# Sparse attention of the odd layer: TensorE in a written order, the score matmuls regrouped by form

## The chip, the cores and the metric

The kernel runs on one core of a Trainium2 chip. The core has five engines that work from instruction queues of their own: TensorE (PE; its weight loads are listed as PEld), VectorE (DVE), ScalarE (ACT), GpSimd (POOL) and SyncE (SP, which here issues DMAs). The metric is the time of one execution on the device in microseconds (us); the median of several runs is quoted.

## The reference, cut to what matters

One sequence of T = 512 tokens, D = 1024, goes through two blocks. The first has two layers, an even one (pool and gated-unit mixer) and an odd one (sparse attention beside retention), each followed by a SwiGLU network; the second has dilated and forgetting attention and a mixture of experts. Only the sparse attention of the odd layer is touched:

```python
def nsa_attention(q, k_cmp, v_cmp, k_sel, v_sel, k_win, v_win, gates, ...):
    # 8 heads in 2 key groups of 4, head dim 64; queries in blocks of 128
    def block(i):                                   # tq: the block's 128 positions
        s = jnp.einsum('bgmqd,bgnd->bgmqn', qb, kc)              # 31 compressed keys
        p_cmp = masked_softmax(s, cmp_end[None, :] <= tq[:, None])
        o_cmp = jnp.einsum('bgmqn,bgnd->bgmqd', p_cmp, vc)
        ...                                          # top 16 blocks of 64 keys
        p = masked_softmax(s, tok_ok)
        o_sel = jnp.einsum('bgmqkl,bgqkld->bgmqd', p, vs)
        ...                                          # window of 512 keys
        o_win = jnp.einsum('bgmqs,bgsd->bgmqd', masked_softmax(s, win_ok), vwb)
        o = jnp.stack([o_cmp, o_sel, o_win], axis=-1)
        return jnp.einsum('bhqdc,bhqc->bqhd', o, gb)
    out = lax.map(block, jnp.arange(t_len // Q_BLOCK))
```

With 512 tokens the 16 chosen blocks and the window of 512 take in every earlier key, so that both branches are causal attention over different keys and values.

## The kernel before, in words

`nsa()` first projects and rotates queries, keys and values, and then runs the attention over `items`, nine for each of four query tiles `qt` of 128 tokens: one `compressed(qt)` and eight `selected(qt, br, b)`, for the two branches `br` (chosen keys, window) and four values of `b`. A selected item covers two heads (one of each key group `g`) and `nk = (qt + 1) * 128` keys: one block of 128 keys in the first tile, four in the last. Each item has three stages.

- `scores()` fills two PSUM tiles `mm` by matmuls: queries against the high part of the keys (`kh`, L840), queries against their low part, a 64-row matmul (`kl`, L844), and a bf16 matmul that adds the causal mask to the last 128 keys (`cmask`, L846). `soft` then has DVE take the row maximum (L892) and ACT the exponential (L902, tile `pe`).
- `turn()` transposes the two `pe` tiles on TensorE, 128x128 at a time (`keys_first`, L914, into PSUM `tp`), and copies them to `pt`, the first on ACT (L919), the second on DVE (L917).
- `values()` multiplies with the values (`pair_av`, L934, 64 columns a matmul) into a PSUM tile `px` that the four items of a branch share. After the fourth, `back()` copies `px` to `nat` on ACT (L940), transposes it by four matmuls on TensorE (L943); DVE scales it (L866, `ot`) and POOL adds it to `o` (L869). After the second branch `to_T` transposes `o` with four more matmuls (L199) and writes `mixa`, which the projection behind the attention reads.

A compressed item has scores on 31 keys (L794), a softmax of several DVE steps and one exponential (tile `ce`), transposes of `ce` (L813) and a matmul with `vbd` (L822) that starts `o`.

`staged()` writes the items with the lags `LAG = (0, 1, 2)`: scores of item n, transposes of n-1, values of n-2. That sets priorities only; a scheduler that works with its own model of durations chooses the order of the instructions on each engine. Every engine then executes its queue in that order, and waits on semaphores for what comes from others. Buffers: four `mm`, two `tp`, two `px` in PSUM, four `pe` and four `pt`.

Late in the last tile the scheduler also has matmuls of the projection behind (on `mixb`, L173 to L175) and the weight splits of the next stage (`whi`, ACT, L149) to place between.

Of the kernel before, what the change touches and what calls it, by code (L numbers as in the profile page):

```python
# [22 lines left out]
P = 128  # L23
# [55 lines left out]

HOLD_N = 8  # L80
UNITS = ("raw",) * 3 + ("more",) * 3 + ("whi", "wlo") * 3
LAG = (0, 1, 2)

QUOTA = ((16, 6.5), (26, 3.75), (35, 2.0))
G_CHUNK = [float(np.exp(P * np.log1p(-np.exp2(-5.0 - h)))) for h in range(4)]
# [6 lines left out]
class Builder:  # L92
# [555 lines left out]
    def nsa(self, np_, cp, h, mixp, mid):  # L648
        nc, A = self.nc, self.A
# [7 lines left out]
        kl = self.t(np_, "nkl", [P, 2, T], F32R)  # L657
# [21 lines left out]
        for tt in range(NT):  # L679
            cs = slice(tt * P, (tt + 1) * P)  # L680
            n = self.t(cp, "nat", [P, 512])
# [16 lines left out]
            for g in range(2):  # L698
                r = slice(64 * g, 64 * g + 64)
# [3 lines left out]
        for tt in range(NT):  # L703
            cs = slice(tt * P, (tt + 1) * P)
            n = self.t(cp, "nat", [P, 512])
# [6 lines left out]
            for g in range(2):  # L712
                r = slice(64 * g, 64 * g + 64)
# [12 lines left out]
        for i, nm in enumerate(("k", "v")):  # L726
# [10 lines left out]
            for lp in range(16):  # L737
                nc.tensor.matmul(ph[i][:, 0:93], w1[:, lp, :], x2[i][:, :, 2 * lp:2 * lp + 481:16], start=lp == 0,
                                 stop=lp == 15)
# [4 lines left out]
        q = self.t(aq, "nq", [P, 8, T], F32R)  # L744
        for tt in range(NT):
            cs = slice(tt * P, (tt + 1) * P)
            n = self.t(aq, "nat", [P, 512])
# [6 lines left out]
            for g in range(2):  # L754
                r = slice(64 * g, 64 * g + 64)
# [72 lines left out]
        def selected(qt, br, b):  # L828

            qs = slice(qt * P, (qt + 1) * P)  # L830
            nk = (qt + 1) * P
            key = (qt, br)
            st = {}

            def scores():
                if b == 0:
                    S[key] = [self.t(at, "sums", [P, 4, 2], bufs=2)]
                ps = [self.ps() for _ in range(2)]
                for g in range(2):
                    nc.tensor.matmul(ps[g][:, :nk], q[:, 4 * g + b, qs], kh[:, 2 * br + g, 0:nk], start=True,  # L840
                                     stop=False)
                for g in range(2):
                    r = slice(64 * g, 64 * g + 64)
                    nc.tensor.matmul(ps[g][:, :nk], q[r, 4 * g + b, qs], kl[r, br, 0:nk], start=False, stop=False)  # L844
                for g in range(2):
                    nc.tensor.matmul(ps[g][:, nk - P:nk], self.identb, self.cmask, start=False, stop=True)  # L846
                st["e"] = [self.soft(at, ps[g], None, nk, S[key][0][:, b, g:g + 1]) for g in range(2)]

            def turn():
                st["et"] = [self.keys_first(at, st["e"][g], nk, g) for g in range(2)]  # L850

            def values():
                if b == 0:
                    S[key].append(self.ps("px"))
                sums, av = S[key]
                self.pair_av(av[:, b * P:(b + 1) * P], st["et"], qt,
                             lambda g, kb: v[:, kb, br, g * 64:(g + 1) * 64])
                if b < 3:
                    return
                o = S[qt]  # L860
                cf = self.t(at, "scf", [P, 4, 2], bufs=2)
                nc.vector.reciprocal(cf, sums)
                nc.vector.tensor_tensor(cf, cf, gate[:, qt, 1 + br:24:3].rearrange("p (g b) -> p b g", g=2), op=ALU.mult)
                po = self.back(aq, av, ("nat", 1))
                t = self.t(at, "ot", [P, 512])
                nc.vector.tensor_tensor(t.rearrange("p (g b n) -> p b g n", g=2, b=4),  # L866
                                        po.rearrange("p (b g n) -> p b g n", g=2, b=4),
                                        cf.unsqueeze(3).to_broadcast([P, 4, 2, 64]), op=ALU.mult)
                nc.gpsimd.tensor_tensor(o, o, t, op=ALU.add)  # L869
                if br == 1:  # L870
                    self.to_T(o, qt, ma)

            return scores, turn, values

        items = []
        for qt in range(NT):
            items.append(compressed(qt))
            items += [selected(qt, br, b) for br in range(2) for b in range(4)]
        self.staged(items)
        self.done(at)  # L880
        self.done(aq)
        self.done(np_)
# [26 lines left out]
    def keys_first(self, pool, e, nk, odd):  # L909
# [8 lines left out]
        else:  # L918
            nc.scalar.activation(et[:, :nk], tp[:, :nk], AF.Copy)  # L919
        return et  # L920

    def staged(self, items, lag=LAG):

        items = list(items)
        for n in range(len(items) + lag[-1]):
            for k, d in enumerate(lag):
                if 0 <= n - d < len(items):
                    items[n - d][k]()

    def pair_av(self, av, et, qt, v):  # L930

# [1089 lines left out]
```

## Time and profile before

| | |
|---|---|
| median of 3 runs | 1884.65 us (1882.86 to 1886.02) |
| profiled execution | 1883.5 us, span 1881.8 us |
| mean granted TensorE clock | 0.971 of full |
| PE busy | 1786.6 us, 95% of the span |
| attention stage on PE, first compressed scores to first `mixa` matmul | 712.4 to 839.6 us |

The profiled execution lies inside the range of the runs, 1.15 us below their median. Times in the trace count from the start of the span. A busy time is the sum over instructions of an engine; matmuls overlap in the pipeline, so the step from the start of one group to the start of the next says what a group costs, and a row's duration is somewhat longer than that step. The granted clock has two levels, 0.50 (1.2 GHz) and 1.00 (2.4 GHz).

### The profile page before, as it was taken

Reading aid. Unit: us, or ns where it says so; the run is one execution under the profiler, and the core shown is the slowest. Engines: PE = TensorE matmul, PEld = TensorE weight load, DVE = VectorE, ACT = ScalarE, POOL = GpSimd, SP = SyncE. Lnnn points to the kernel's source line nnn. Section 1 sums busy time; section 2 is a strip of 40 time slices with the busy share of each in tenths; the row PEclk is TensorE's granted clock in tenths of the full one; section 3 lists DMA queues with packets and bytes.
Section 4 is the critical chain, followed back from the end, with each engine's and each line's share of the span. In section 5 each row is a group of like instructions: output and inputs, shape, how many; then the busy total and the mean of one; then the engine's idle time right before and its main releaser. Section 6 shows DMA issues by size and latency. Waiting matters only on the chain. (4 is left out here: it accounts for less than half of the span.)

```text
span 1881.8 us, 23441 instructions
## 1 busy us (share of the span) xinstructions
PE 1786.6 (95%) x9314; PEld 1367.1 (73%) x9315; DVE 922.6 (49%) x1637; ACT 626.5 (33%) x1152; POOL 164.6 (9%) x312
## 2 busy tenths in 40 slices
PE   8999999999999999999999999998999976999997
PEld 6788888888799876778888888876876763444443
DVE  7654444444645345555444444465455563334334
ACT  6333222222431334554322222245556421111112
POOL 1001000000232110002000000020000121000000
PEclk9999999999999996999999999999999986999999
DMA  6433223222331301043232232242312294999972
GB/s 231 148 134 132 93 90 105 97 90 90 111 125 56 90 25 44 1 144 103 90 112 90 90 111 90 68 140 87 92 46 83 80 339 176 374 369 376 348 305 86
DMA packets 136308, 257.01 MB, mean 137 GB/s; under 512 B 11319, under 2 KB 88023, under 8 KB 131971
## 3 DMA queue, kind: packets, MB, share of 16 engines
q1 hardware_dynamic: 124000, 231.89, 35.5%
q10 hardware_dynamic: 9282, 13.10, 2.1%
q0 software_dynamic: 2912, 10.49, 1.4%
q8 instruction: 75, 1.23, 0.3%
q14 instruction: 39, 0.31, 0.0%
HBM read 247.04 MB, written 11.03 MB: 137 GB/s over the span
## 5 line engine op out<-in xcount | busy, mean ns | idle before, releaser
L173 PE MATMUL mm<-acth,whi 128*128 128x512 f32 (+2 forms) x968 | 368.9, 381 | 0.0
L174 PE MATMUL mm<-actl,whi 128*128 128x512 f32 (+2 forms) x968 | 365.0, 377 | 0.0
L175 PE MATMUL mm<-acth,wlo 128*128 128x512 f32 (+2 forms) x968 | 364.4, 376 | 0.0
L150 DVE TENSOR_TENSOR wlo<-raw,whi 128x2048 fp32r<-128x2048 f32 (+1 forms) x96 | 218.7, 2279 | 247.6 <-ACT whi L149 247.4
L149 ACT ACTIVATE whi<-raw 128x2048 fp32r<-128x2048 f32 (+1 forms) x96 | 182.5, 1901 | 435.0 <-issue 195.2
L173 PEld LDWEIGHTS mm<-acth,whi 128*128 128x128 f32 (+1 forms) x968 | 182.0, 188 | 35.2 <-issue 2.4
L175 PEld LDWEIGHTS mm<-acth,wlo 128*128 128x128 f32 (+1 forms) x968 | 182.0, 188 | 34.5 <-issue 0.2
L174 PEld LDWEIGHTS mm<-actl,whi 128*128 128x128 f32 (+1 forms) x968 | 182.2, 188 | 33.6 <-issue 1.0
L173 PE MATMUL mm<-whi,acth 128*128 128x256 f32 (+2 forms) x480 | 160.2, 335 | 2.1 <-ACT gate L707 1.7
L174 PE MATMUL mm<-wlo,acth 128*128 128x256 f32 (+2 forms) x480 | 158.1, 330 | 0.6 <-DVE wlo L150 0.6
L175 PE MATMUL mm<-whi,actl 128*128 128x256 f32 (+2 forms) x448 | 145.6, 327 | 0.4 <-DVE actl L204 0.3
L173 PE MATMUL px<-whi,hidh 128*128 128x512 f32 x352 | 137.4, 390 | 0.6 <-DVE macc L331 0.6
L175 PE MATMUL px<-whi,hidl 128*128 128x512 f32 x352 | 137.9, 392 | 0.0
L174 PE MATMUL px<-wlo,hidh 128*128 128x512 f32 x352 | 137.4, 390 | 0.0
L331 DVE TENSOR_TENSOR macc<-px,macc 128x512 f32<-128x512 f32 x144 | 97.6, 688 | 75.3 <-PE px L175 75.3
L173 PEld LDWEIGHTS mm<-whi,acth 128*128 128x128 f32 x480 | 91.4, 191 | 10.2 <-ACT gate L707 1.9
L174 PEld LDWEIGHTS mm<-wlo,acth 128*128 128x128 f32 x480 | 91.2, 190 | 8.4 <-DVE wlo L150 1.3
L175 PEld LDWEIGHTS mm<-whi,actl 128*128 128x128 f32 x448 | 85.1, 190 | 7.2 <-DVE actl L204 1.0
L173 PEld LDWEIGHTS px<-whi,hidh 128*128 128x128 f32 x352 | 66.1, 188 | 16.4 <-DVE macc L331 1.5
L311 DVE TENSOR_TENSOR hidf<-mm,silu 128x512 f32<-128x512 f32 x44 | 30.4, 690 | 94.8 <-PE mm L175 94.8
L175 PEld LDWEIGHTS px<-whi,hidl 128*128 128x128 f32 x352 | 66.1, 188 | 14.1 <-DVE hidl L313 0.5
L174 PEld LDWEIGHTS px<-wlo,hidh 128*128 128x128 f32 x352 | 66.1, 188 | 13.2
(427 smaller groups left out, 2683.8 us busy)
## 6 DMA issues: line engine op xcount, KB each, us to landing
raw<-in_ffn_w_gate SPq DMA_DIRECT2D x22, 1024.0 KB, 5.2
raw<-in_ffn_w_up SPq DMA_DIRECT2D x22, 1024.0 KB, 5.3
raw<-in_ffn_w_down SPq DMA_DIRECT2D x22, 1024.0 KB, 4.8
mixd<-in_w_expert_down SPq DMA_DIRECT2D x16, 1024.0 KB, 6.9
down<-in_w_expert_down SPq DMA_DIRECT2D x16, 1024.0 KB, 9.1
raw<-in_od_w_in SPq DMA_DIRECT2D x12, 1024.0 KB, 5.0
raw<-in_w_expert_gate SPq DMA_DIRECT2D x18, 512.0 KB, 8.4
raw<-in_w_expert_up SPq DMA_DIRECT2D x18, 512.0 KB, 8.3
```

Source lines behind the costliest of these rows:

```text
L149: self.nc.scalar.activation(hi[:, :n], raw[:, :n], AF.Copy)
L150: self.nc.vector.tensor_tensor(lo[:, :n], raw[:, :n], hi[:, :n].bitcast(F32), op=ALU.subtract)
L173: mm(out, l[0], r[0], start=first, stop=False)
L174: mm(out, l[0], r[1], start=False, stop=False)
L175: mm(out, l[1], r[0], start=False, stop=last)
L311: nc.vector.tensor_tensor(hf, pu[f], s, op=ALU.mult)
L331: nc.vector.tensor_tensor(m, p, m, op=ALU.add)
```

## The change

In `scores()` the two mask matmuls come between those of the high part and those of the low part, which are now last. The items are written out under a manual schedule for PE: TensorE's instructions are executed in exactly the order in which the code writes them. In step n that order is the transposes of item n-2, the scores of item n, and the values of item n-2. `staged` and `LAG` go. The orders of DVE and ACT are still chosen by the scheduler, around the new order of PE; the orders of SP and POOL are the same rows as before. Lines move by a few: `kh` L839, `cmask` L842, `kl` L845, exponential L908, transposes L920, `pt` L923 and L925, values L932, `nat` L938, `back` L941, `to_T` L198, `ce` transposes L812.

```diff
@@ scores
                 for g in range(2):
+                    nc.tensor.matmul(ps[g][:, nk - P:nk], self.identb, self.cmask, start=False, stop=False)
+                for g in range(2):
                     r = slice(64 * g, 64 * g + 64)
-                    nc.tensor.matmul(ps[g][:, :nk], q[r, 4 * g + b, qs], kl[r, br, 0:nk], start=False, stop=False)
-                for g in range(2):
-                    nc.tensor.matmul(ps[g][:, nk - P:nk], self.identb, self.cmask, start=False, stop=True)
+                    nc.tensor.matmul(ps[g][:, :nk], q[r, 4 * g + b, qs], kl[r, br, 0:nk], start=False, stop=True)
@@ the loop over the items
-        self.staged(items)
+        with self.tc.manual_schedule(engines={mybir.EngineType.PE}):
+            for n in range(len(items) + 2):
+                if n >= 2:
+                    items[n - 2][1]()
+                if n < len(items):
+                    items[n][0]()
+                if n >= 2:
+                    items[n - 2][2]()
@@ gone
-LAG = (0, 1, 2)
-    def staged(self, items, lag=LAG):
-        items = list(items)
-        for n in range(len(items) + lag[-1]):
-            for k, d in enumerate(lag):
-                if 0 <= n - d < len(items):
-                    items[n - d][k]()
```

**The end of a first branch.** The first place is TensorE in the third tile (three blocks of keys), where the first branch (`br` 0) ends. Before, behind the last values of that branch (into `px_6364`), these rows stood:

```order
L840 MATMUL mm_6487<-nkh_4825,nq_5552 128x384
L840 MATMUL mm_6488<-nkh_4825,nq_5552 128x384
L844 MATMUL mm_6487<-nkl_4826,nq_5552 128x384
L844 MATMUL mm_6488<-nkl_4826,nq_5552 128x384
L846 LDWEIGHTS identb_79
L846 MATMUL mm_6487<-cmask_81,identb_79 128x128
L846 LDWEIGHTS identb_79
L846 MATMUL mm_6488<-cmask_81,identb_79 128x128
L914 MATMUL tp_6503<-ident_72,pe_6449 128x128 x3
L943 MATMUL px_6479<-ident_72,nat_6477 128x128 x4
L914 MATMUL tp_6509<-ident_72,pe_6453 128x128 x3
```

Now the same place, from the last two of the branch's last six values matmuls (into `px_6354`) on; ahead of the six stand the `kl` scores of `mm_6442` and `mm_6443`:

```order
L932 MATMUL px_6354<-pt_6434,v_4827 64x128
L932 MATMUL px_6354<-pt_6440,v_4827 64x128
L941 MATMUL px_6469<-ident_72,nat_6467 128x128 x4
L920 MATMUL tp_6477<-ident_72,pe_6417 128x128 x3
L920 MATMUL tp_6483<-ident_72,pe_6421 128x128 x3
L839 MATMUL mm_6489<-nkh_4825,nq_5552 128x384
L839 MATMUL mm_6490<-nkh_4825,nq_5552 128x384
```

The transposes of `back` (of `nat`) stood a whole scores group and three transposes behind the values whose result they need; now they stand directly behind them. The same has happened at the ends of the other branches.

**The end of a tile.** The second place is TensorE at the end of the second branch of the same tile, where `o` (`o_6014` before, `o_6006` now) is finished. Before:

```order
L943 MATMUL px_6288<-ident_72,nat_6286 128x128 x4
L822 MATMUL px_6332<-vbd_5487,ct_6277 128x256 x2
L840 MATMUL mm_6337<-nkh_4825,nq_5552 128x384
L844 MATMUL mm_6337<-nkl_4826,nq_5552 128x384
L846 LDWEIGHTS identb_79
L846 MATMUL mm_6337<-cmask_81,identb_79 128x128
L840 MATMUL mm_6371<-nkh_4825,nq_5552 128x384
L840 MATMUL mm_6372<-nkh_4825,nq_5552 128x384
L199 MATMUL tp_6296<-ident_72,o_6014 128x128 x4
L914 MATMUL tp_6319<-ident_72,pe_6267 128x128 x3
```

Now:

```order
L932 MATMUL px_6172<-pt_6252,v_4827 64x128
L932 MATMUL px_6172<-pt_6257,v_4827 64x128
L941 MATMUL px_6285<-ident_72,nat_6283 128x128 x4
L198 MATMUL tp_6293<-ident_72,o_6006 128x128 x4
L812 MATMUL tp_6300<-ident_72,ce_6234 128x128 x2
L839 MATMUL mm_6305<-nkh_4825,nq_5552 128x384
```

The transposes of `o` stood six matmuls of the next tile and the values of its compressed item behind those of `nat`; now nothing stands between them. The same holds at the end of the first two tiles; at the end of the last tile the `mixb` matmuls of the projection still stand between.

**The copy that `back` waits for.** The third place is ACT around the copy `nat` at the first place. Now:

```order
L925 ACTIVATE pt_6434<-tp_6430 128x384
L908 ACTIVATE pe_6451,sums_6407<-mm_6442,nm_6450 128x384
L908 ACTIVATE pe_6455,sums_6407<-mm_6443,nm_6454 128x384
L938 ACTIVATE nat_6467<-px_6354 128x512
L925 ACTIVATE pt_6481<-tp_6477 128x384
```

The copy `nat` stands behind both exponentials of the scores `mm_6442` and `mm_6443`, which TensorE computes directly before the last values. Before, `nat_6477` stood behind the two exponentials of the preceding scores in the same way.

## Rows read from the trace of the kernel before

**Rows 1.** The page, part 1: busy time, share of the span, instructions.

```profile
PE 1786.6 (95%) x9314; PEld 1367.1 (73%) x9315; DVE 922.6 (49%) x1637; ACT 626.5 (33%) x1152; POOL 164.6 (9%) x312
```

**Rows 2.** Windows of the stage: length; busy PE, PEld, DVE, ACT, POOL; granted clock; DMA.

```profile
712.30:729.30 17.00, 13.88 (x58) 11.34 (x58) 11.40 (x38) 7.92 (x23) 0.00 (x0) 0.50 0.12 44
729.40:739.50 10.10, 10.07 (x83) 7.30 (x82) 4.80 (x21) 5.97 (x28) 1.26 (x1) 1.00 0.01 2
739.60:753.10 13.50, 13.50 (x53) 8.95 (x51) 6.97 (x18) 5.38 (x18) 1.27 (x1) 0.50 0.00 0
753.30:839.60 86.30, 84.93 (x676) 61.61 (x676) 52.00 (x102) 47.64 (x123) 7.69 (x6) 1.00 0.21 73
```

**Rows 3.** Waits of PE in the stage: line and releaser, us in total, times, longest.

```profile
PE tp L199 <- POOL o L869: 1.1, 3, 0.6
```

**Rows 4.** Timeline of PE, one item of three blocks: start, us, work [idle before].

```profile
783.52 0.61 PE L840 MATMUL mm<-nkh,nq 128*128 128x384 f32 x2
784.07 0.44 PE L844 MATMUL mm<-nkl,nq 64*128 64x384 f32 x2
784.45 0.29 PE L846 MATMUL mm<-cmask,identb 128*128 128x128 bf16 x2
784.57 0.82 PE L914 MATMUL tp<-ident,pe 128*128 128x128 f32 x6
785.32 0.88 PE L934 MATMUL px<-pt,v 128*64 128x128 f32 x12
786.13 0.44 PE L840 MATMUL mm<-nkh,nq 128*128 128x384 f32 x1
```

**Rows 5.** Timeline of PE where scores follow transposes.

```profile
761.15 0.60 PE L914 MATMUL tp<-ident,pe 128*128 128x128 f32 x4
761.51 0.36 PE L840 MATMUL mm<-nkh,nq 128*128 128x256 f32 x1
```

**Rows 6.** Timeline of DVE and ACT beside and behind rows 4.

```profile
784.71 1.02 DVE L892 TENSOR_REDUCE nm<-mm 128x1 f32<-128x384 f32 x2 [1.12 <-PE mm L846]
785.55 0.57 ACT L902 ACTIVATE pe<-mm,nm 128x384 f32<-128x384 f32 x1
786.10 0.58 ACT L902 ACTIVATE pe<-mm,nm 128x384 f32<-128x384 f32 x1
786.66 0.60 ACT L940 ACTIVATE nat<-px 128x512 f32<-128x512 f32 x1
```

**Rows 7.** Timeline of PE at a tile's end, transposes of `nat` and of `o`.

```profile
771.95 0.60 PE L943 MATMUL px<-ident,nat 128*128 128x128 f32 x4
774.77 0.44 PE L199 MATMUL tp<-ident,o 128*128 128x128 f32 x2 [0.24 <-POOL o L869]
```

**Rows 8.** Timeline of PE, from one compressed item's values to the next's.

```profile
772.39 1.03 PE L822 MATMUL px<-vbd,ct 128*128 128x256 f32 x4
791.77 1.96 PE L794 MATMUL mm<-kcT,nq 128*128 128x32 f32 x16
799.47 0.38 PE L822 MATMUL px<-vbd,ct 128*128 128x256 f32 x1
```

**Rows 9.** Timeline of PE at the start of the stage.

```profile
723.88 0.47 PE L840 MATMUL mm<-nkh,nq 128*128 128x128 f32 x1 [3.06 <-ACT pe L902]
```

**Rows 10.** Timeline of PE: the same scores at either clock level.

```profile
740.33 0.80 PE L840 MATMUL mm<-nkh,nq 128*128 128x256 f32 x2
758.28 0.50 PE L840 MATMUL mm<-nkh,nq 128*128 128x256 f32 x2
```

**Rows 11.** Timeline and windows around two stretches where PE stood idle.

```profile
1639.54 0.63 PE L1675 MATMUL tp<-ident,xg 128*128 128x128 f32 x4 [1.06 <-ACT wsl L1650]
1640.70:1644.00 3.30, 3.14 (x10) 1.48 (x12) 0.20 (x1) 0.70 (x2) 0.00 (x0) 0.50 0.96 307
666.00:668.00 2.00, 0.31 (x2) 0.22 (x2) 1.97 (x2) 1.70 (x3) 1.71 (x1) 1.00 0.00 0
668.00:675.00 7.00, 6.28 (x36) 4.85 (x35) 5.57 (x28) 3.10 (x12) 2.20 (x6) 1.00 0.42 150
```

## The prediction

> **What bounds the kernel now.** I read the page first: TensorE (PE) is busy for 95% of the span [rows 1], so time is won or lost where PE's groups get shorter or where PE stands still. Then the windows of the attention stage, which alone is touched. PE is granted half of its clock for the first 17 us, the full clock for 10, half again for 13.5, and the full clock for the last 86.3, of which it is busy 84.93 [rows 2]. So before the change PE hardly waits in the stage, although every item passes through DVE and ACT between its matmuls; the waits of PE name only the transposes of `o`, 1.1 us in three places [rows 3]. Last the timeline of one item of three blocks: from one score group to the next are 2.61 us: high part 0.55, low part 0.38, mask 0.12, transposes 0.75, values 0.81 [rows 4]. That is matmul after matmul, and the other engines' work lies under it.
>
> **The regrouping.** No matmul is added or removed; only neighbours change. In rows 4 the six transposes take 0.75 us up to the values, which are about 0.11 a step and 0.20 for the last, since a matmul of another shape of the array (64 columns) follows. Where high-part scores follow four transposes, the four take 0.36 [rows 5], three steps of 0.11 and a last one of 0.03. In the new order scores follow the transposes in every item: minus 0.17. The transposes now follow the values instead of the mask; I take 0.05 more for that, an estimate from the first step of the values, which is longer by about as much than the later ones. The mask followed by another score group instead of transposes: about minus 0.02. Sum minus 0.14 us an item, and about the same at one, two and four blocks since only borders change: 32 items, **minus 4.4 us** (bounds minus 5, without the 0.05 and a little more, and minus 1, if the low part pays at its border with the values what the transposes saved).
>
> A page bears on this. The Trainium skill, "TensorEngine Tiling (Array Packing)", section "Key Properties", says that a change of the tiling mode drains TensorE. An item had four such changes and has three, so by the page one border an item goes, which at the 0.09 us by which the border step exceeds the others would be minus 2.9 us, between my bounds. The row does not show a drain as such, only the longer step.
>
> **The written order at the ends of branches.** This is the large term. Before, the transposes of `nat` stood a score group and some transposes behind the values that they wait for, and PE did not wait there; now they stand directly behind. In the new order ACT copies `nat` behind both exponentials of the scores that PE finishes just before these values. For three blocks, counted from the start of the values, t: the first maximum can start when the low part ends, t + 0.06; one maximum is 0.51 (half of the pair's 1.02), and with 0.14 to the exponential, an estimate, the first exponential starts at t + 0.71; the two exponentials take 0.55 each from start to start, and `nat` starts at t + 1.81; its 0.60 and an estimated 0.07 to PE give t + 2.48 [rows 6]. PE is through the values at t + 0.81 [rows 4]. It waits 2.48 - 0.81 = 1.67 us. With fewer keys the exponentials and the values both get shorter; I work out 1.4 for one block and 1.6 for two, and 2.1 for four, where a weight split of ACT can stand between: **6.8 us for the four first branches**. At the ends of the first three tiles the scores ahead are the next tile's and one exponential fewer stands ahead of `nat`: I take 0.85, 1.35 and 1.35, **3.5 us**. At the end of the last tile matmuls of the projection still cover it, at nothing; without that cover it would be another 1.5.
>
> Behind `back`, at the ends of the first three tiles, PE comes at once to the transposes of `o`. These wait for DVE's scaling and POOL's addition. Before, from the start of the transposes of `nat` to those of `o` passed 2.82 us, of which PE waited 0.24, since it had the compressed values and scores to do meanwhile [rows 7]. That time was set by POOL, so it stays; PE's own part of it is now the four transposes alone, 0.44 (771.95 to 772.39, [rows 7, 8]). It waits 2.82 - 0.44 = 2.38 us, three times: **7.1 us**. The matmuls that covered it still have to be done afterwards. Stalls together **plus 17.4 us** (bounds 13.6, with each `nat` a row of 0.55 earlier and nothing at the first tile, and 19).
>
> **What the written order removes.** The waits of 0.24 and its like at the ends of the first three tiles are inside the 2.82 now: **minus 0.5 us** (the last tile's 0.6 stays). And the scheduler's order was irregular at the ends of tiles, with single score matmuls between others. From the values of one compressed item to the next in the third tile pass 27.08 us (772.39 to 799.47). Eight items of 2.61 make 20.9, the scores of the compressed item 1.9, its transposes and values 0.9, two backs 0.9, the transposes of `o` 0.45, and 0.6 more for the scores of the next tile that fall inside with four blocks: 25.7 [rows 4, 7, 8]. The 1.4 left over, three times, is **minus 4.2 us** (bounds minus 6 and 0, if the surplus belongs to the work and not to its order).
>
> **The start.** Before, PE had scores of two and a half items to do before it stood still for 3.06 us on the exponentials that free its buffers [rows 9]; in the new order it has one item's scores and then the transposes of `ce`, behind the softmax of the compressed item. Both orders wait for that chain. The scores that were done early come later: one and a half items at one block, at half clock about 1 us each, **plus 1.5 us** (bounds 0 and plus 3).
>
> **The clock.** The same pair of scores takes 0.80 us at half and 0.50 at full clock [rows 10], a ratio of 1.6. The half stretch of 13.5 us [rows 2] thus costs 13.5 x (1 - 1/1.6) = 5.1 us. An idle time of 1.06 us late in the kernel is followed by some 3.4 us at half clock, which by the same ratio costs 1.3; but an idle time of 1.69 us (most of the window from 666 to 668) is followed by the full clock [rows 11]. Seven stalls of the new order could each bring such a stretch, plus 9; or the stretch of 13.5 us may not come back, minus 5. The rows bear out both kinds; I take **plus 2 us**, near the middle.
>
> **The sum.** -4.4 + 17.4 - 0.5 - 4.2 + 1.5 + 2 = +11.8 us on the profiled 1883.5: **1895 us**, slower by 0.6%. The profiled execution lies 1.15 us below the median of its runs, so that on the median the sum would be 1896.5; I stay with 1895.
>
> **Rivals.** What a measurement of this kernel can tell from no change is about 0.2%, 3.8 us.
>
> 1. *PE does not stand still at the moved transposes, and the kernel is faster.* If ACT and DVE run so far ahead of PE that `nat` and `o` are ready in time, the stalls fall away and the sum is -5.6: about 1878 us, or 1871 if the half stretch goes too. It decides if the stalls are below 5.6 us. For it: ACT is busy for 47.64 of 86.3 us [rows 2] and could copy `nat` earlier. Against it: the order has `nat` behind both exponentials, and POOL's addition was waited for even with cover [rows 3]. The Trainium skill ("TensorE: Matmul & The Clock Gate", section "Part 3: Packing small matmuls — row/col tiling") says that matmuls keep strict program order; the trace agrees as far as PE stood idle 0.24 us before the transposes of `o`. Chance 0.08.
> 2. *The clock stays full* from 729 on, in spite of the stalls: -5.1 in place of +2, 1888 us. For it: the stalls are short and the idle of 1.69 us did no harm [rows 11]. Chance 0.15.
> 3. *The stalls hold the clock down*: the full stretch of 10.1 us [rows 2] at half, 10.1 x 0.6 = +6.1, and half stretches behind most stalls, +3.5 more: 1905 us. For it: the stalls in the first two tiles come while the clock goes up and down anyway. Chance 0.14.
> 4. *The regrouping saves nothing*: stalls as forecast, 1899.5 us. As a mechanism: the weights of the first scores cannot be loaded under the last transpose, so that the border costs what the border to the values cost. The 0.03 in rows 5 speak against it. The same page and section of the Trainium skill have weight loads overlap running matmuls only where the row group differs, which is not so between transposes and scores; that is this rival, and row and rule differ here. Chance 0.06.
>
> **How the numbers follow.** The forecast has 0.57; its own range, from the bounds of stalls, surplus and start, is 1889 to 1901. The range of 1886 to 1905 leaves out the first rival and about half of the third, and a little of the forecast: 0.2. Faster than 1881 us: the first rival, 0.08. Within 0.2%, up to 1888.4: rather more than half of the second and a little of the forecast, 0.13. Slower: 0.79.
>
> **What would show it.** In the new profile the seven transposes of `nat` outside the last tile's end should have idle time before them released by ACT (`nat`), 1.3 to 2.1 us at first branches, and the transposes of `o` three waits on POOL of 2.2 to 2.5 us; PE's waits in the stage should come to some 17 us more than before. Six transposes followed by scores should take about 0.6 us, an item of three blocks 2.46. From the values of the third tile's compressed item to those of the fourth's [rows 8] should pass some 3 us more. I am wrong above all if `nat` is ready much sooner than t + 2.48, if the scheduler's surplus was worth more than 4 us, or if the clock in the first two tiles goes another way.

## The result, and the profile after

The changed kernel took 1903.04 us (median of 5 runs, 1894.88 to 1905.46) against 1884.2 us before (median of 5 too, the three of the table ahead and two more): 18.8 us more between the medians. The ratio over all runs is 1.0081, 95% interval 1.0063 to 1.0100, which is 12 to 19 us. Runs of either kernel scatter by several us with the granted clock (one set of 30 runs of the kernel before goes from 1881.6 us at a mean of 0.973 to 1892.3 at 0.965, and 1894.88 us is the one run of the changed kernel at 0.971, the other four being at 0.965), so kernels are compared below by the ratio to runs of the kernel before on the same chip.

The page of the changed kernel, part 1, answers to [rows 1]:

```profile
PE 1791.6 (94%) x9314; PEld 1371.8 (72%) x9315; DVE 926.6 (49%) x1637; ACT 626.7 (33%) x1152; POOL 162.4 (9%) x312
```

The same matmuls are busy for 5 us more in a span that is 21.7 us longer (1903.5): PE stands still more, and its matmuls are on the mean slower. Where it waits says the view of PE's waits in the attention stage (line and releaser, us in total, times, longest), which answers to [rows 3]:

```profile
PE px L941 <- ACT nat L938: 10.0, 7, 2.5
PE tp L198 <- POOL o L868: 7.1, 4, 2.2
PE tp L812 <- ACT ce L801: 4.1, 1, 4.1
```

Seven waits on `nat` and four on the sum `o`; the fourth of the latter, 0.6 us, was there before. The third row is the wait at the start, which was 3.06 us before [rows 9]. How fast PE ran shows in the windows of the stage (columns as in [rows 2], which they answer to):

```profile
55.30:62.10 6.80, 6.80 (x17) 4.39 (x15) 6.37 (x7) 0.60 (x1) 0.22 (x3) 0.50 0.44 157
717.50:761.80 44.30, 36.14 (x173) 28.25 (x173) 21.18 (x65) 16.95 (x61) 2.53 (x2) 0.50 0.02 8
761.90:785.70 23.80, 18.89 (x174) 14.57 (x172) 13.31 (x35) 11.81 (x42) 2.53 (x2) 1.00 0.00 1
785.80:789.10 3.30, 3.30 (x12) 2.50 (x11) 2.28 (x4) 1.51 (x6) 0.00 (x0) 0.50 0.00 0
789.20:816.40 27.20, 22.08 (x214) 17.02 (x212) 15.74 (x35) 13.49 (x39) 2.54 (x2) 1.00 0.01 2
816.50:819.80 3.30, 3.30 (x11) 1.88 (x11) 1.98 (x3) 1.35 (x3) 0.00 (x0) 0.50 0.00 0
819.90:860.30 40.40, 37.22 (x290) 27.44 (x289) 22.91 (x31) 20.67 (x42) 2.58 (x2) 1.00 0.42 149
```

The clock is at half from the start of the stage to the end of the first tile, 44.3 us in one piece; the full stretch of 10 us that stood between two half ones in [rows 2] is gone. Half stretches come again behind the waits at the ends of the second and the third tile. The first row lies far ahead of the stage and is one of the clock's changes from run to run (below).

The stage itself, from the first compressed scores to the first `mixa` matmul, runs from 716.4 to 860.4 us, these rows of PE's timeline:

```profile
716.37 0.28 PE L793 MATMUL mm<-kcT,nq 128*128 128x32 f32 x1 [0.56 <-ACT kcT L767]
...
860.40 0.39 PE L172 MATMUL mm<-whi,mixa 128*128 128x512 f32 x1
```

It takes 144.0 us, and took 127.2 (712.4 to 839.6): 16.8 of the 22.0 us between the two profiled executions (1905.46 and 1883.5). PE's busy time in it is the second number of these windows, the first of the kernel before and the second of the changed one:

```profile
712.40:839.60 127.20, 122.74 (x866) 89.29 (x867) 75.27 (x177) 66.95 (x190) 10.23 (x8) 0.88 0.16 55
716.40:860.40 144.00, 121.99 (x867) 92.51 (x868) 78.52 (x177) 66.71 (x190) 10.18 (x8) 0.82 0.14 48
```

PE is busy for as long as before and stands idle for 22.0 us where it was 4.5.

One item of three blocks gives the answer to [rows 4]:

```profile
791.12 0.88 PE L920 MATMUL tp<-ident,pe 128*128 128x128 f32 x6
791.75 0.60 PE L839 MATMUL mm<-nkh,nq 128*128 128x384 f32 x2
792.19 0.28 PE L842 MATMUL mm<-cmask,identb 128*128 128x128 bf16 x2
792.40 0.44 PE L845 MATMUL mm<-nkl,nq 64*128 64x384 f32 x2
792.77 0.88 PE L932 MATMUL px<-pt,v 128*64 128x128 f32 x12
793.58 0.88 PE L920 MATMUL tp<-ident,pe 128*128 128x128 f32 x6
```

From transposes to transposes 2.46 us, where it was 2.61: in step starts, 0.63 for the six transposes and their border to the scores (0.75 before).

The chain behind a first branch's last values, with the same columns, on three engines; it answers to [rows 6]:

```profile
797.70 0.88 PE L932 MATMUL px<-pt,v 128*64 128x128 f32 x12
797.80 1.02 DVE L898 TENSOR_REDUCE nm<-mm 128x1 f32<-128x384 f32 x2 [0.28 <-PE mm L845]
798.45 0.58 ACT L908 ACTIVATE pe<-mm,nm 128x384 f32<-128x384 f32 x1 [0.84 <-DVE nm L898]
799.02 0.57 ACT L908 ACTIVATE pe<-mm,nm 128x384 f32<-128x384 f32 x1
799.58 0.59 ACT L938 ACTIVATE nat<-px 128x512 f32<-128x512 f32 x1
800.23 0.66 PE L941 MATMUL px<-ident,nat 128*128 128x128 f32 x4 [1.65 <-ACT nat L938]
```

PE's values end at 798.6; `nat` could be copied from then on, but ACT has two exponentials ahead of it in its queue, the first of which waits for DVE. PE comes to the transposes 2.53 us after the values began.

The end of a tile, the answer to [rows 7]:

```profile
812.87 0.66 PE L941 MATMUL px<-ident,nat 128*128 128x128 f32 x4 [1.27 <-ACT nat L938]
813.64 0.69 DVE L865 TENSOR_TENSOR ot<-px,scf 128x512 f32<-128x512 f32 x1 [1.32 <-PE px L941]
814.41 1.26 POOL L868 TENSOR_TENSOR o<-o,ot 128x512 f32<-128x512 f32 x1 [11.38 <-DVE ot L865]
815.72 0.55 PE L198 MATMUL tp<-ident,o 128*128 128x128 f32 x3 [2.19 <-POOL o L868]
```

From one group of transposes to the other 2.85 us, 2.82 before, and now all but PE's own part of it is idle.

### The profile page after: what moved, and what is told of

It reads as the page before. It is cut to its first block, busy times and chain, and to the rows that moved or that the text cites. A ratio compares the mean times of both kernels' runs of the same rounds, so it can differ in the third digit from the quotient of the medians.

```text
span 1903.5 us, 23434 instructions
## 1 busy us (share of the span) xinstructions
PE 1791.6 (94%) x9314; PEld 1371.8 (72%) x9315; DVE 926.6 (49%) x1637; ACT 626.7 (33%) x1152; POOL 162.4 (9%) x312
## 4 chain that ended last, share of the span: by engine, by line
PE 26%; issue 20%; DVE 3%; ACT 2%; POOL 1%; DMA 0%; POOLq 0%; ACTq 0%; DVEq 0%
PE mm L1686 5%; PE mm L1709 4%; PE px L1727 3%; PE mm L172 3%; PE mm L174 3%; PE mm L173 3%; PE px L932 1%; PE tp L920 1%; PE tp L1673 1%; PE sc L1198 1%; PE sc L1192 1%; POOL rq L214 0%; DMA xg<-hd,ix 0%; DVE hn L240 0%; PE tp L1639 0%
```

## The experiments

**The changed kernel again**, unaltered.

> The changed kernel once more, beside the others of this call on the same chip: 1895 to 1906 us, as in its five runs. The first profile has 16.8 of its 22 us in the attention stage and 4 us ahead of it, where no instruction differs. Theory: the 4 us are the clock's (6.8 us at half clock near 55 us) and differ from run to run; rival: they belong to the change and come again.

1901.82 us (5 runs), ratio 1.0070 (1.0046 to 1.0093). The stage begins at 711.97 us, not at 716.37, and takes 143.0 us: the 4 us ahead of the stage do not belong to the change (the half stretch of 6.8 us there is worth 2.6 of them by the forecast's ratio), and some 16 us in the stage do. The clock in the first tile is not the same as in the first profile of this kernel:

```profile
712.00:729.00 17.00, 12.36 (x56) 10.48 (x56) 10.98 (x35) 7.25 (x18) 0.00 (x0) 0.50 0.11 42
729.10:735.80 6.70, 4.86 (x47) 3.51 (x43) 2.65 (x13) 4.22 (x20) 0.00 (x0) 1.00 0.00 1
735.90:756.30 20.40, 17.48 (x83) 13.53 (x82) 8.94 (x24) 6.45 (x25) 2.53 (x2) 0.50 0.00 1
```

Here the full clock came back for 6.7 us, and fell again behind the wait of 1.39 us on `nat` that ended at 735.15 us. Half clock in the whole stage comes to some 48 us here, 51 in the first profile and 31 before.

**Only the regrouping**, with the scheduler's order: the edit of `scores()` in the diff, made in the kernel before.

> The kernel before, with only the mask matmuls moved ahead of the low part; the scheduler chooses the order. The number of borders between array shapes stays the same in that order, four an item (high to low part, low part to transposes, transposes to values, values to scores), so my theory gives no change: 1882 to 1886 us. Rival (the regrouping itself saves, or costs, at every item): 4 us or more to either side.

1883.55 us, ratio 0.9994 (0.9978 to 1.0010): no change, as expected. In the scheduler's order the regrouping bought nothing.

**Only the written order**:

```diff
+                    r = slice(64 * g, 64 * g + 64)
+                    nc.tensor.matmul(ps[g][:, :nk], q[r, 4 * g + b, qs], kl[r, br, 0:nk], start=False, stop=False)
+                for g in range(2):
+                    nc.tensor.matmul(ps[g][:, nk - P:nk], self.identb, self.cmask, start=False, stop=True)
```

in place of the mask first and the low part last.

> The changed kernel with the mask matmuls last again, as before; only the written order. My theory: one border more an item (low part to mask, mask to values), +0.09 to 0.14 us for 32 items, so 3 to 4.5 us above the changed kernel: 1904 to 1908 us. Rival (the saving comes from the transposes being followed by scores alone, the place of the mask is worth nothing): within 1.5 us of the changed kernel.

1898.25 us (4 runs, 1895.96 to 1905.8), ratio 1.0062 (1.0037 to 1.0087), not to be told from the changed kernel's 1.0070, and below the expected range. The rows of PE's timeline still show the border:

```profile
788.40 0.87 PE L920 MATMUL tp<-ident,pe 128*128 128x128 f32 x6
...
789.94 0.29 PE L845 MATMUL mm<-cmask,identb 128*128 128x128 bf16 x2
790.15 0.88 PE L932 MATMUL px<-pt,v 128*64 128x128 f32 x12
790.96 0.33 PE L920 MATMUL tp<-ident,pe 128*128 128x128 f32 x1
```

An item takes 2.56 us, 0.10 more than with the mask first, 3.2 us over 32 items. The waits on `nat` are 8.3 us here instead of 10.0, which gives back half of it, and the rest is inside the scatter. The time cannot decide, the rows can: of the 0.15 us an item that the change gains, the written order alone has 0.05, and the mask's new place on top of it has 0.10.

**Transposes of `nat` and of `o` later** (both), and **those of `nat` alone** (the list `late` is worked off behind the values of each step; cut to what matters):

```diff
-                po = self.back(aq, av, ("nat", 1))
+                def finish():
+                    po = self.back(aq, av, ("nat", 1))
...
+                late.append((1, finish))                              # behind the next item's values
                 if br == 1:
-                    self.to_T(o, qt, ma)
+                    late.append((2, lambda: self.to_T(o, qt, ma)))    # nat alone: 1
```

> Keeps the written order and the regrouped scores, but writes the transposes of nat one item later (behind the next item's values) and those of o one item later again. Stall theory: the waits before them (6.8 + 3.2 + 6.6 us in the changed kernel's trace) go almost wholly, and some half-clock time with them; what is left is the regrouping (-4.4) and the regular order (-4.2, perhaps less) against before: 1874 to 1881 us. Rival (the written order is slow as such, or the half clock of the first two tiles comes from elsewhere): 1886 to 1892 us, with the waits gone from the trace all the same.

> As the run with both late, but the transposes of o stay directly behind those of nat. Stall theory: the waits on nat go, the three waits on POOL of 2.2 us stay, so about 6.6 us above the run with both late, more by 1 to 3 if they bring half clock: 1881 to 1890 us. Rival (only nat's wait matters, the POOL wait is covered once nat is early): the same time as both late.

Both late: 1883.19 us, ratio 0.9996 (0.9978 to 1.0014), all of the loss gone but nothing gained. `nat` alone: 1895.05 us, ratio 1.0043 (1.0022 to 1.0063), above the expected 1881 to 1890 us. PE's waits with both late:

```profile
PE tp L812 <- ACT ce L801: 5.6, 2, 4.1
PE tp L935 <- ACT pt L940: 3.1, 3, 1.3
PE tp L198 <- POOL o L870: 0.9, 2, 0.6
PE px L821 <- ACT ct L815: 0.9, 1, 0.9
```

The waits on `nat` are gone, and on `o` 0.4 us are left besides the old 0.6. In their place stand 3.1 us on `pt` and more on `ce` and `ct`, at the ends of tiles: the transposes of `o` hold one of the two `tp` tiles just when the next item's transposes want two. These waits are the likely reason that it missed my 1874 to 1881 us, though no run shows that they are the whole of it: the stage itself takes 123.7 us, 3.6 less than before, of which the medians show 1.5. The second run, against the first, puts a price on a wait: 7.5 us on POOL instead of 0.9, with 1.2 us less on `pt`, and 11.9 us more time between the medians (8.9 by the ratios). Its windows show what the rest is:

```profile
742.10:755.60 13.50, 10.63 (x46) 7.90 (x46) 5.23 (x12) 4.22 (x15) 1.26 (x1) 0.50 0.00 1
755.80:776.10 20.30, 17.06 (x152) 13.10 (x152) 12.57 (x33) 10.97 (x38) 2.53 (x2) 1.00 0.00 1
776.20:782.90 6.70, 6.06 (x34) 4.49 (x32) 2.27 (x4) 2.62 (x7) 0.00 (x0) 0.50 0.00 0
...
807.00:813.60 6.60, 5.85 (x32) 3.96 (x31) 2.67 (x4) 2.43 (x5) 0.00 (x0) 0.50 0.00 0
```

The waits on POOL end at 775.8 and 806.4 us, and behind each follows a half stretch of 6.7 us; with both late there was half clock only up to 745.9 us. In the whole stage it comes to some 44 us, and to 20 with both late.

**The waits filled**: useless transposes of the identity in front of the real ones, 8 or 4 for `nat`, 12 for `o`.

```diff
         po = self.ps("px")
+        for _ in range(fill):
+            self.nc.tensor.transpose(po[:, 0:P], self.ident, self.ident)
```

> The changed kernel with useless transposes of the identity ahead of those of nat (8 at first branches, 4 at the ends of three tiles) and of o (12), into the PSUM tile that the real ones overwrite: TensorE works where it stood still, and nothing that it waits for comes sooner. Stall theory with the clock as a part of the price: less half clock in the stage (51 us in the profile of the changed kernel, before 31), so 4 to 9 us below the changed kernel: 1893 to 1899 us. Rival (the price is the waits alone): no faster than the changed kernel, 1901 to 1906 us, since at half clock the fill lasts longer than some waits.

1890.97 us, ratio 1.0019 (1.0000 to 1.0037): 10.9 us below the changed kernel on the same chip between the medians (9.6 by the ratios), more than I had expected. PE's timeline, at the place of the chain above:

```profile
790.65 0.88 PE L934 MATMUL px<-pt,v 128*64 128x128 f32 x12
791.45 1.09 PE L943 MATMUL px<-ident 128*128 128x128 f32 x8
793.17 0.33 PE L945 MATMUL px<-ident,nat 128*128 128x128 f32 x1 [0.62 <-ACT nat L940]
```

From the values to the transposes of `nat` 2.52 us, as before the fill (2.53), and at the end of the same tile 2.85 us from those of `nat` to those of `o`, as in the changed kernel: at these places nothing that PE waits for came sooner. The fill covers the waits in part; 3.9 us on `nat` and 2.3 on POOL are left. The windows of the same run:

```profile
715.70:742.90 27.20, 23.10 (x113) 18.72 (x115) 13.90 (x46) 11.21 (x38) 0.77 (x1) 0.50 0.03 11
743.00:746.40 3.40, 3.39 (x33) 2.82 (x30) 1.76 (x8) 1.95 (x10) 0.40 (x1) 1.00 0.02 5
746.50:753.20 6.70, 6.70 (x34) 5.41 (x34) 3.41 (x10) 2.09 (x7) 0.58 (x1) 0.50 0.00 0
753.30:851.00 97.70, 91.18 (x766) 69.47 (x765) 57.87 (x111) 50.60 (x134) 8.25 (x7) 1.00 0.18 59
```

After 753.3 us the clock stays full to the end of the stage. So what the fill bought is the clock. By the medians that was more than half of the loss, 10.9 of 13.6 us on this chip; the two profiles taken there show less, 5.8 us of 15.8 in the stage (137.2 against 143.0). The filled kernel's profiled execution took 1896.93 us, 6 more than its median, so the profile cannot show the rest.

**Earlier places** (the `late` list is worked off ahead of the values, delays 0 and 2), and on top of it **the compressed item early**, whose edit is shown:

```diff
-            items.append(compressed(qt))
             items += [selected(qt, br, b) for br in range(2) for b in range(4)]
+        for qt in range(NT):
+            items.insert(max(9 * qt - 1, 0), compressed(qt))
```

> As both late, but the transposes of nat come before the next item's values instead of behind them, and those of o before the values two items later, so that they no longer hold a tp tile while the next transposes want two. The waits on pt and ct of the run with both late (3.8 and 0.9 us) should go, and about 4 us with them: 1876 to 1880 us. Rival (those waits only move, ACT being late with its queue at the tile ends): 1881 to 1885 us.

> As the run with early places, with the compressed item of the next tile written one item earlier, ahead of the last selected item, so that its softmax has an item more of time. The wait of 1.5 us on ce at the first tile's end should go: 1 to 2 us below the run with early places, 1875 to 1879 us. Rival (ce is hidden but ACT's copy for it meets the exponentials): no difference.

1884.13 us, ratio 0.9981 (0.9966 to 0.9997), and 1882.42 us, ratio 0.9977 (0.9963 to 0.9992), both above what I had expected. The first halved the waits on `pt` (1.6 us) but has 3.4 us on `nat` again: the rival was right, the waits moved. The second took 1.0 us from the wait on `ce`; the 1.7 us between the two medians are inside the scatter.

**That kernel again, with its start filled, and with scores at its start**: 16 useless transposes ahead of the first transposes of `ce`; or the third step's scores written ahead of its transposes.

> The run with the compressed item early once more, beside the two others of this call: 1880 to 1885 us, 2 to 6 us below the kernel before on the same chip, as in its first twelve runs; if it does not beat the kernel before again, that first result was the chip's.

> As the run with the compressed item early, with 16 useless transposes of the identity ahead of the first transposes of ce, where TensorE stands still for 4.1 us at half clock. Clock theory: the full clock comes back sooner (after some 10 us in place of 13.7 to 17) and 1 to 3 us go: 1878 to 1882 us. Rival (the fill itself, 3.5 us at half clock, only takes the place of the wait and the clock comes back when it did): no change.

> As the run with the compressed item early, with the second selected item's scores written ahead of the first transposes of ce, so that TensorE has work in the wait of 4.1 us, as the scheduler had it. My theory of the start (plus 1.5 us for what is no longer done early): 1 to 1.5 us less than with the compressed item early. Rival: the compressed values, now directly behind the transposes of ce, wait for their copy ct instead, 0.5 to 1 us, and nothing is left.

1883.58 us, ratio 0.9993 (0.9976 to 1.0011); 1881.84 us, 0.9989 (0.9976 to 1.0001); 1883.9 us, 0.9990 (0.9978 to 1.0003). Against the kernel before, the gain of the first is unclear: 0.9977 in one set of runs and 0.9993 in the other, 1 to 4 us. Its stage takes 122.3 and 120.9 us in the two profiles, 5 to 6 less than before, so in the stage the written order does save; the profiled executions as a whole are only 1.5 and 2.6 us shorter, with 3 to 7 us more of half clock behind the stage. With the start filled, the windows show the full clock back after some 10 us of half clock, where the repeated run without the fill had half from 713.5 to 730.4 (and the first run of that kernel for 13.6 us):

```profile
713.50:723.60 10.10, 9.88 (x47) 9.47 (x47) 7.69 (x24) 4.01 (x6) 0.00 (x0) 0.50 0.13 48
723.70:737.20 13.50, 11.64 (x97) 9.03 (x98) 6.93 (x27) 7.95 (x38) 1.27 (x1) 1.00 0.01 2
737.40:744.10 6.70, 6.67 (x30) 4.88 (x28) 3.88 (x14) 2.91 (x12) 0.00 (x0) 0.50 0.00 0
```

It falls again at 737.4 us, as it does in the first profile without the fill at 738.3, and the 1.7 us between the two medians are inside the scatter. The scores at the start gained nothing: their wait on `ce` is 3.3 us instead of 4.1, but the compressed values wait 0.6 us on `ct`, as the rival had it.

## Why the prediction was right, and which terms were off

The forecast was slower, 1895 us within 1886 to 1905; 1903 is inside, near the upper end. The range that the forecast's own terms gave was 1889 to 1901, and 1903 is beyond it: the stated range holds it only because it was stretched for the third rival, and that is luck as far as the sum goes. The main mechanism, stalls at the moved transposes that outweigh the regrouping, was right; two terms were off, the clock above all.

The windows of the stage give the balance. PE is idle for 17.5 us more (22.0 against 4.5), and half clock costs 5.8 more (worked out below); of 16.8 us in all that leaves the work itself 6.5 us shorter. The forecast had 16.9 and 1.5 for idle time and start, 2 for the clock and 8.6 for the work.

- **Waits at moved transposes**, forecast 17.4 us. On `nat`, first branches: 1.15, 1.47, 1.65 and 2.53, 6.8 us together (forecast 6.8; the first is shorter since PE was at half clock, and in the repeated run, at full clock there, it is 1.39); at tile ends 0.72, 1.25 and 1.27, 3.2 us (forecast 3.5); on `o` three times 2.19, 6.6 us (forecast 7.1). Sum 16.6. The sum of the first branches agrees better than its parts, the last of which was forecast 2.1. The chain came at t + 2.53 against t + 2.48, and the 0.14 and 0.07 us in it that the forecast took without a row came to 0.14 (797.80 + 0.51 to 798.45) and 0.06 (799.58 + 0.59 to 800.23).
- **Regrouping**, forecast -4.4: an item of three blocks came to the forecast 2.46 us. The rows bear out the parts too: the transposes went from 0.75 to 0.63, minus 0.12 as forecast (0.17 less 0.05), and the three score groups together from 1.05 to 1.02, minus 0.03 where I had 0.02. The runs of each half alone add that the two parts lean on each other: with the mask last, its border to the values takes 0.21 us where its border to the transposes took 0.12, so that the order alone gains 0.05 an item, and the regrouping alone, in the scheduler's order, gained nothing.
- **What the order removes**, forecast -4.7: from the third tile's compressed values to the fourth's passed 31.94 us (786.41 to 818.35) against 27.08 in [rows 8], 4.9 more. With 5.1 us of waits, eight items shorter by 0.15 and some 4.6 us of half clock at 0.375 each (1.7), the surplus that went is 27.1 + 5.1 - 1.2 + 1.7 - 31.9 = 0.8 us there, where I had 1.4. The old wait of 0.24 us is a part of this 0.8, and of my 1.4 too, so that the forecast, which took the waits off by themselves as well, counted them twice (0.5 us). In three tiles that makes about 2.4 in place of 4.7. No run tested this term alone.
- **The start**, forecast +1.5: not told apart. The wait there is 4.1 us in place of 3.06, the first compressed values came 0.75 us sooner after the stage's start than before, and the run with scores at the start gave nothing back.
- **The clock**, forecast +2: this is the term that was mis-sized most. In half clock PE was busy for 36.14 + 3.30 + 3.30 = 42.7 us of the changed profile, and for 13.88 + 13.50 = 27.4 before [rows 2]; 15.4 us more at 1 - 1/1.6 make 5.8 us. The terms then give -4.4 + 16.6 - 2.4 + 1.5 + 5.8 = 17.1, against the 16.8 us measured. In the repeated run PE was busy at half clock for 38.8 us, which makes 4.2. I weighed a stall by whether a short half stretch follows it. What happened lies between that +2 and the third rival (chance 0.14, 9.6 us for the clock): in the first tile the full stretch went in one profile and was cut to 6.7 us in the other, and in the later tiles half stretches came behind the waits on POOL, not behind most stalls. The filled run puts the clock higher, 10.9 us between the medians (9.6 by the ratios), of which the two profiles show 5.8 in the stage; where the rest lies is open. That the stalls are what held the clock down in the first tile is not shown, since before the change it fell there too, with PE busy [rows 2].

The first rival fell: PE stood idle at each of the ten moved groups that the forecast named. The second fell with the half stretches. The fourth fell too: the saving is in the rows, though no run shows it in the time by itself. The forecast's opening remark that PE's waits name only the transposes of `o` leaves out the 3.06 us of [rows 9], which it uses further on; no term hangs on it.

The Trainium skill, "TensorE: Matmul & The Clock Gate", section "Part 3: Packing small matmuls — row/col tiling", has weight loads overlap running matmuls only where the row group differs; elsewhere the same section also lets a load into the background weight buffer go ahead. By the first of these sentences the border from transposes to scores should have saved nothing. The trace has six transposes and that border in 0.63 us, 0.17 for the first step, 0.11 for each of the next four and 0.03 for the last, which starts here and the scores at 791.75 (above):

```profile
791.72 0.27 PE L920 MATMUL tp<-ident,pe 128*128 128x128 f32 x1
```

So the measurement decides against that sentence for this border. The Trainium skill, "TensorEngine Tiling (Array Packing)", section "Key Properties", says that a change of mode drains TensorE, and gives no figure. The forecast's estimate for one border saved was 0.09 us, from [rows 4]; the mask's place, which is one change of mode an item, measured 0.10, and the trace agrees as far as such a border costs time.

## What to carry to other kernels

When an order is written by hand, every instruction that waits for another engine needs its own place in it: a transposition that stands directly behind the values it comes from stops TensorE for the whole round trip, here 0.7 to 2.5 us, and moving it one item later gives that back, until it meets the next limit (here the two `tp` tiles). Price a TensorE stall at more than its length where matmuls fill the time around it: 6.6 us of waits on POOL cost 9 to 12 us here, and behind those that came at the full clock the clock fell. Filling such a stall with useless matmuls is a quick way to find out how much of a loss is the clock's, if it is read from many runs, since the clock differs from run to run.

## What the runs showed of the hardware

PE met eight waits of 2.2 to 2.4 us on POOL at the full clock, two in each profile of the changed kernel, of the written order alone and of `nat` alone; each time the clock fell to half during the wait or within 1.3 us of its end, and stayed there for 3.3 to 6.7 us. Other waits went either way. One of 1.47 us on `nat` was followed by the full clock in the changed kernel (it ended at 771.18 us) and by half clock in the run with the written order alone:

```profile
764.90 0.66 PE L941 MATMUL px<-ident,nat 128*128 128x128 f32 x4 [1.47 <-ACT nat L938]
765.70:768.90 3.20, 3.20 (x19) 2.22 (x18) 1.78 (x4) 1.30 (x5) 1.27 (x1) 0.50 0.02 5
```

The longest, 2.53 us on `nat` in the last tile, was followed by the full clock in both profiles of the changed kernel; in that run its like, 2.41 us, was not. So the length of a wait does not say by itself what the clock does. Nor does the clock need a wait to fall: before the change it fell at 739.6 us behind 10.1 us of which PE was busy for 10.07 [rows 2]. With the waits filled it stayed full from 753.3 us to the end of the stage.

I had expected short half stretches, at 1.3 us each, but not that the first tile, with waits of 1.2 and 0.7 us on `nat`, would go with a half stretch of 44.3 us in one piece, which the repeated run did not show either. With the start filled the half stretch ended after 10.1 us in place of 16.9, which I had expected; that the clock fell again at 737.4 us I had not. What makes it fall in the first tile stays open.
